# A hybrid encoder layer on one core: modulation matmuls with their operands exchanged, and the stores of summed MLP weight quarters moved from ScalarE's queue to GpSimd's

## The chip, the core and the metric

The kernel is one program on one core of a Trainium2 chip. The time is the device time of one execution in microseconds: 2640.66 us, the median of three runs (2637.92 to 2642.81). A core has five engines that run side by side and meet at semaphores: TensorE (PE; its weight loads are listed as PEld), VectorE (DVE), ScalarE (ACT), GpSimd (POOL) and SyncE (SP), which here only issues DMAs. Each engine takes its instructions strictly in the order in which they stand. DMAs are issued by SP, ACT and POOL.

## The reference

One encoder layer over a prompt of 2048 positions and a sample of 512, width 1024, all in float32:

```
mod = silu(c) @ w_ada + b_ada            # 6 x 1024 values for each of the two requests
shift1, scale1, gate1, shift2, scale2, gate2 = split(mod, 6)
z   = (rmsnorm(x) * (1 + scale1) + shift1) @ w_in
y_f = per-head maps of Re(FFT2(z[:, :512])) + b          # Fourier heads
y_s = GLU(GELU(S5 scan, both ways, of z[:, 512:]))       # state-space heads
x   = x + gate1 * (concat(rmsnorm(y_f), rmsnorm(y_s)) @ w_out)
h   = rmsnorm(x) * (1 + scale2) + shift2
y   = rmsnorm(x + gate2 * (square(relu(h @ w_mlp_in + b)) @ w_mlp_out + b))
```

Two parts matter here. `mod` is a product of a 1024 x 6144 matrix with only two vectors, one per request. The MLP's two products, 1024 x 4096 and 4096 x 1024, are the bulk of the work.

## The kernel before

Most products keep float32 accuracy by splitting both operands into a high and a low part in float32r and adding three products (`mm3`, lines 230 to 232). The modulation, the scan and its outputs use plain float32 matmuls, which the chip runs as two instructions each: the profile shows two records for one matmul in the code.

The stages in order of time, as the profile shows them: the first 2048 columns of the modulation and the parameters of the scan, the input projection and its Fourier folds (to about 340 us); the scan (`Ssm`) with the Fourier transform and its output projection beside it (to about 660 us); the gated unit, the rest of the output projection and the residual (`mix_out`, to about 1010 us); the MLP.

*Modulation slots.* The last 4096 columns of the modulation are 32 blocks j = 16 to 47 of 128 columns. The loop over groups of the scan calls `slot` between its steps; a slot does one block (`ada_slot`, `ada`) and then a unit of the Fourier work. Weights `wa` are loaded two blocks ahead. In `ada`, a block is 8 matmuls (line 688), each with a 128 x 128 block of `w_ada` as the loaded operand and the 128 x 2 tile `cs` of silu(c) as the moved one, summed in a 128 x 2 PSUM tile `pa`; VectorE adds the bias into `mod[:, j]` (line 689). The first 16 blocks are done at the start by `ada1`, with the operands the other way round: `cs` is loaded (two columns), 512 columns of weights are moved (line 706), the 2 x 512 result is copied out by ScalarE into `ar` (line 708) and turned by four small transposes `pat` (line 711).

*Sums of weight quarters.* The MLP uses a scheme of seven products with seven half-size weight matrices for eight. Four of its factors are sums of quarters of a weight matrix, the same in every run but made by the kernel. `precombine` makes one sixteenth of a matrix: SP loads four tiles of 128 x 512 (`in_w`, line 1259), GpSimd makes four sums in place (line 1264), and each sum is stored to `wS` in HBM (line 1265), the store issued by ScalarE. 20 of the 32 calls stand in `mix_out`, with one buffer for each of the four tiles (`q`), and 12 in the first 60 steps of the MLP, in a scratch three calls deep (`big`). The MLP's weight loads `wr` (line 1398) come from the inputs or from `wS`, are cast by ScalarE to high parts `wh` (line 1408), and VectorE makes the low parts `wl` (line 1410).

GpSimd also raises row sums to the power -1/2 for each norm (line 751) and squares the MLP's hidden values (line 1435).

The order in which instructions stand on each engine is set by a scheduler which simulates the program as it is recorded. It works with costs of its own, and its order stands from then on.

Of the kernel before, what the change touches and what calls it, by code (L numbers as in the profile page):

```python
# [9 lines left out]
F32 = mybir.dt.float32  # L10
F32R = mybir.dt.float32r
# [6 lines left out]
LP, LS = 2048, 512  # L18
# [215 lines left out]
def ssm_pre(net, P, pm, side, A, sI, sT, job):  # L234


    nc, tc = net.nc, net.tc
    s4 = [128, NQ, 16, 8]
    flat = lambda t: t.rearrange("p h t -> p (h t)")
    with tc.tile_pool(name="pre1", bufs=1, side=side) as tm, tc.tile_pool(name="pre2", bufs=1, side=side) as tp:  # L240
        T = lambda n, sh=s4, tag=None, bufs=2: tp.tile(sh, F32, tag=tag or n, name=n, bufs=bufs)
        newTh = lambda: tm.tile([128, 2 * NQ, 16, 8], F32, name="Th", bufs=1)
        Th = newTh()
        shf = tm.tile([128, 15, 128], F32R, name="shf")
        net.gate(shf[:1, 0, 0:1])
        nc.gpsimd.dma_start(shf, A["shm"])

        ccs = [{k: T("CC%d%s" % (i, k), [128, NQ, 2, 16], bufs=1) for k in "ri"} for i in range(CB)]
        for cc in ccs:
            for k in "ri":  # L250
                nc.gpsimd.memset(cc[k], 0.0)
        for q in range(32 // NQ):
            gs = slice(q * NQ, q * NQ + NQ)
            if q % 2 == 0:

                Mh = [[tm.tile([128, 2 * NQ, 16], F32R, name="Mh%d%d" % (d, i), bufs=1) for i in range(2)] for d in range(2)]
            ms = slice(q % 2 * NQ, q % 2 * NQ + NQ)
            cc = ccs[q % CB]
            for k, c in (("r", P["Cr"]), ("i", P["nCi"])):
                for d in range(2):  # L260
                    nc.scalar.copy(cc[k][64 * d:64 * d + 64, :, d], c[64 * d:64 * d + 64, gs])
            I = {k: T("I" + k) for k in "ri"}
            pw = {k: bc(P["PWi"][k][:, gs].unsqueeze(2), s4) for k in "ri"}
            bb = {k: bc(P["Bb"][k][:, gs].unsqueeze(3), s4) for k in "ri"}
            for e, k, x, y, op in ((nc.gpsimd, "r", "r", "i", ALU.subtract), (nc.vector, "i", "i", "r", ALU.add)):
                t = T("cb" + k, bufs=1)
                e.tensor_tensor(I[k], bb["r"], pw[x], op=ALU.mult)
                e.tensor_tensor(t, bb["i"], pw[y], op=ALU.mult)
                e.tensor_tensor(I[k], I[k], t, op=op)
            for c, k in enumerate("ri"):  # L270
                It = T("It", [128, NQ, 128])
                ps = net.ps([128, 4, 128], "pst")
                for j in range(4):
                    nc.tensor.transpose(ps[:, j], flat(I[k][:, j]), net.ident)
                nc.scalar.copy(It, ps)
                nc.scalar.dma_start(sI[q, :, c], It)
            ps = net.ps([128, NQ, 2, 16], "psm")
            for j in range(NQ):
                for k in "ri":
                    nc.tensor.matmul(ps[:, j].rearrange("p d h -> p (d h)"), flat(I[k][:, j]), cc[k][:, j].rearrange("p d h -> p (d h)"), start=k == "r", stop=k == "i")  # L280
            M = T("M", [128, 2, NQ, 16])
            Dm = T("Dm", [128, NQ, 16])
            nc.sync.dma_start(Dm, A["s_d"][gs].partition_broadcast(128))
            nc.vector.tensor_tensor(Dm, Dm, bc(P["msk"].unsqueeze(1), [128, NQ, 16]), op=ALU.mult)
            nc.vector.tensor_tensor(M[:, 0], ps[:, :, 0], Dm, op=ALU.add)
            nc.scalar.copy(M[:, 1], ps[:, :, 1])
            for d in range(2):
                split(nc, Mh[d][0][:, ms], Mh[d][1][:, ms], M[:, d])
            job(q)
            for _ in range(2):  # L290
                net.ada_slot()
            if q % 2 == 0:
                continue
            if q > 1:
                Th = newTh()
            for t0 in (0, 4):
                ps = net.ps([128, 4, 2 * NQ, 16], "psT")
                for tau in range(t0, t0 + 4):
                    for d, o in ((0, 14), (1, 7)):
                        for i in range(2):  # L300
                            nc.tensor.matmul(ps[:, tau - t0], shf[:, o - tau], Mh[d][i], start=d + i == 0, stop=d + i == 2)
                nc.scalar.copy(Th[:, :, :, t0:t0 + 4], ps.rearrange("p t g h -> p g h t"))
            for i in range(2):
                nc.scalar.dma_start(sT[q - 1 + i], Th[:, i * NQ:i * NQ + NQ].rearrange("p g h t -> p g (h t)"))


def ssm_out(net, P, tp, q, sO):
# [253 lines left out]
class Net:  # L561
# [3 lines left out]
    def run(self):  # L565
        tc, nc, A = self.tc, self.nc, self.A
        with ExitStack() as es:
# [23 lines left out]
            spps, spp = pool("spp", "right")  # L591
            fes, fe = pool("fe", "right")
            self.Ze = [fe.tile([96, n], F32R, name="Ze%d" % n) for n in (352, 256)]
            self.aj, self.wa = 16, {}
            self.pcs = [(w, c) for w in range(2) for c in range(16)]
            P = self.mix_in(spp)
            sas, sa = pool("ssa", "right")
# [6 lines left out]
            for q in range(nb + 2):  # L604
                if q < nb:
                    bl.append(S.lead(q))
                    self.slot(gen)
                if 1 <= q <= nb:
                    S.step2(bl[q - 1])
                if q >= 2:  # L610
                    self.slot(gen)
                    S.step3(bl[q - 2])
                    self.slot(gen)
                if q < nb:
                    S.step1(bl[q])
                    self.slot(gen)
            self.pull(gen, 1000)
            self.banks(7)
            sps.close()
# [61 lines left out]

    def ada(self, j):
        nc = self.nc
        v3 = lambda n: self.v[n].unsqueeze(2).broadcast_to([128, 8, 2])
        ps = self.ps([128, 2], "pa")
        w = self.wa.pop(j)
        for k in range(8):
            nc.tensor.matmul(ps, w[:, k], self.cs[:, k], start=k == 0, stop=k == 7)  # L688
        nc.vector.tensor_scalar(self.mod[:, j], ps, self.v["b_ada"][:, j:j + 1], None, op0=ALU.add)
        if j == 39:  # L690
            nc.vector.scalar_tensor_tensor(self.gs2, self.mod[:, 32:40], 1.0, v3("g_mlp_norm"), op0=ALU.add, op1=ALU.mult)
        if j == 47:
            nc.vector.tensor_scalar(self.ng2, self.mod[:, 40:48], -1.0, None, op0=ALU.mult)
            nc.vector.tensor_tensor(self.gb2, self.mod[:, 40:48], v3("b_mlp_out"), op=ALU.mult)
# [277 lines left out]
    def fourier(self):  # L972
# [3 lines left out]
        tc, nc, A = self.tc, self.nc, self.A  # L976
        v = nc.vector
        with ExitStack() as es:
            P = lambda n: es.enter_context(tc.tile_pool(name=n, bufs=1))
            tt = P("ft")  # L980
# [3 lines left out]
            CW3 = tp.tile([96, 512], F32R, name="cw3")  # L984
            Z = [t0.tile([128, 4, 352], F32R, name="Z%d" % x) for x in range(2)]
            part = lambda n: tt.tile([128, 516], F32, tag="zin", name="zin", bufs=2)[:, :n]
            zz = t0.tile([128, 94], F32, name="zz")
            v.memset(zz, 0.0)
            for z in Z:
                nc.scalar.copy(z[:, :, 258:352], bc(zz.unsqueeze(1), [128, 4, 94]))  # L990
            lines = [self.fourier_line(tt, tp, CW, CW3, L, ts, Z if L == LP else [t0.tile([128, 1, 352], F32R, name="Zs%d" % x) for x in range(2)], part, zz) for L, ts in self.SEQ]
            def maps():
                wf = tp.tile([128, 4, 128], F32, tag="yF", name="wfo", bufs=YF)
                nc.sync.dma_start(wf, A["w_f"])
# [18 lines left out]
                    else:  # L1013
                        lines.remove(g)

    def fourier_line(self, tt, tp, CW, CW3, L, ts, Z, part, zz):
        nc, A = self.nc, self.A
        v = nc.vector
        q, nt, o = L // 4, len(ts), 128 * 4 * ts[0]
        tag = "p" if L == LP else "s"  # L1020
        T = lambda n, sh, bufs=1, pool=tp: pool.tile(sh, F32R, tag=tag + n, name=n, bufs=bufs)
        if L != LP:
            for z in Z:
                nc.scalar.copy(z[:, 0, 258:352], zz)
        for par in range(2):
# [222 lines left out]
    def precombine(self, pt, bufs=2):  # L1248

        nc = self.nc  # L1250
        if not self.pcs:
            return
        w, c = self.pcs.pop(0)
        A = self.A["w%d" % (w + 1)]
        cc, hf = c // 2, slice(512 * (c % 2), 512 * (c % 2) + 512)
        T = (lambda n, i: pt.tile([128, 512], F32, tag=n, name=n, bufs=bufs)) if not callable(pt) else pt
        a11, a12, a21, a22 = (T(n, i) for i, n in enumerate(("q0", "q1", "q2", "q3")))
        for j, t in enumerate((a11, a12, a21, a22)):
            nc.sync.dma_start(t, A[j, cc, :, hf])
        e = nc.gpsimd  # L1260
        S = self.wS[w]
        for j, o, x, y, op in ((0, a22, a21, a22, ALU.add), (2, a21, a11, a21, ALU.subtract),
                               (1, a11, a22, a11, ALU.subtract), (3, a12, a12, a11, ALU.subtract)):
            e.tensor_tensor(o, x, y, op=op)  # L1264
            nc.scalar.dma_start(S[j, cc, :, hf], o)

    def mlp(self):
        tc, nc, A = self.tc, self.nc, self.A
# [285 lines left out]
```

## Time and profile before

| | |
|---|---|
| median of three runs | 2640.66 us (2637.92 to 2642.81) |
| the profiled execution | 2639.52 us, its span 2637.8 us |
| TensorE busy | 2521.1 us, 96% of the span |
| VectorE, ScalarE busy | 1723.8 us (65%), 1292.3 us (49%) |
| GpSimd busy | 491.3 us (19%) |

Busy time is a share of the span and says nothing of the speed of the work: TensorE's clock has two levels, 1.2 and 2.4 GHz, and the profile gives the granted clock of a stretch as a share of the upper one, so 0.50 is the lower level. An engine's idle time counts only if what it waits for lies on the path to the end. A name like `L688` is line 688 of the kernel; `out<-in` are the tiles it writes and reads; `x16` is the number of records.

### The profile page before, as it was taken

Reading aid. Unit: us, or ns where it says so; the run is one execution under the profiler, and the core shown is the slowest. Engines: PE = TensorE matmul, PEld = TensorE weight load, DVE = VectorE, ACT = ScalarE, POOL = GpSimd, SP = SyncE. Lnnn points to the kernel's source line nnn. Section 1 sums busy time; section 2 is a strip of 40 time slices with the busy share of each in tenths; the row PEclk is TensorE's granted clock in tenths of the full one; section 3 lists DMA queues with packets and bytes.
Section 4 is the critical chain, followed back from the end, with each engine's and each line's share of the span. In section 5 each row is a group of like instructions: output and inputs, shape, how many; then the busy total and the mean of one; then the engine's idle time right before and its main releaser. Section 6 shows DMA issues by size and latency. Waiting matters only on the chain.

```text
span 2637.8 us, 35325 instructions
## 1 busy us (share of the span) xinstructions
PE 2521.1 (96%) x12643; PEld 2280.8 (86%) x12643; DVE 1723.8 (65%) x2839; ACT 1292.3 (49%) x2267; POOL 491.3 (19%) x406
## 2 busy tenths in 40 slices
PE   6789899999989999899999999999999999999997
PEld 2678778778767878799999999999999999999997
DVE  7888778776539767868677877563446442634454
ACT  2643356564524435636544557265445572654443
POOL 4410010000445440951300003013000020130000
PEclk8889978979899999999999999999999999999998
DMA  8644476455678976887666767676667666766664
GB/s 296 204 149 114 138 244 219 166 177 172 210 273 266 310 265 235 291 289 262 235 218 233 270 245 248 234 279 228 228 225 277 243 246 228 274 232 223 224 224 164
DMA packets 274432, 610.53 MB, mean 231 GB/s; under 512 B 66000, under 2 KB 110096, under 8 KB 272464
## 3 DMA queue, kind: packets, MB, share of 16 engines
q1 hardware_dynamic: 233808, 532.35, 59.3%
q10 hardware_dynamic: 34096, 61.32, 6.2%
q0 software_dynamic: 6352, 14.60, 1.7%
q8 instruction: 100, 1.64, 0.2%
q14 instruction: 76, 0.62, 0.1%
HBM read 452.32 MB, written 155.85 MB: 231 GB/s over the span
## 4 chain that ended last, share of the span: by engine, by line
PE 69%; DVE 12%; DMA 9%; ACT 4%; issue 3%; POOL 3%; SPq 0%; ACTq 0%; DVEq 0%; POOLq 0%
PE acc L232 9%; PE acc L231 9%; PE acc L230 9%; PE pf L231 9%; PE pf L230 9%; PE pf L232 9%; PE pa L688 2%; PE psY L383 2%; POOL q L1264 2%; DMA xq<-in_xq 2%; DMA q<-in_w 1%; PE psV L351 1%; DMA wS<-q 1%; PE pof L230 1%; PE pof L231 1%
## 5 line engine op out<-in xcount | busy, mean ns | idle before, releaser
L1408 ACT CAST wh<-wr 128x512 fp32r<-128x512 f32 x672 | 413.7, 620 | 684.9 <-PE acc L231 347.1
L230 PE MATMUL pf<-th,wh 128*128 128x426 f32 (+1 forms) x1344 | 480.6, 358 | 5.0 <-ACT wh L1408 3.9
L232 PE MATMUL pf<-th,wl 128*128 128x426 f32 (+1 forms) x1344 | 476.5, 357 | 8.0 <-DVE wl L1410 8.0
L231 PE MATMUL pf<-th,wh 128*128 128x426 f32 (+1 forms) x1344 | 480.3, 357 | 1.4 <-DVE th L1358 1.4
L231 PE MATMUL acc<-th,wh 128*128 128x426 f32 (+1 forms) x1344 | 478.4, 357 | 0.4 <-DVE th L1358 0.3
L230 PE MATMUL acc<-th,wh 128*128 128x426 f32 (+1 forms) x1344 | 474.5, 357 | 0.0
L232 PE MATMUL acc<-th,wl 128*128 128x426 f32 (+1 forms) x1344 | 466.9, 357 | 2.1 <-DVE wl L1410 2.0
L1428 DVE TENSOR_TENSOR big<-big,pf 128x426 f32<-128x426 f32 (+1 forms) x320 | 184.4, 594 | 179.5 <-PE pf L232 152.9
L1410 DVE TENSOR_TENSOR wl<-wr,wh 128x512 fp32r<-128x512 f32 x288 | 227.2, 800 | 88.4 <-ACT wh L1408 88.0
L1358 DVE TENSOR_TENSOR th<-big,th 128x1704 fp32r<-128x1704 f32 (+1 forms) x82 | 158.7, 1935 | 185.4 <-ACT th L1357 185.2
L232 PEld LDWEIGHTS pf<-th,wl 128*128 128x128 f32 x1344 | 253.0, 188 | 19.2 <-DVE wl L1410 10.5
L230 PEld LDWEIGHTS pf<-th,wh 128*128 128x128 f32 x1344 | 253.0, 188 | 16.0 <-ACT wh L1408 5.3
L232 PEld LDWEIGHTS acc<-th,wl 128*128 128x128 f32 x1344 | 253.1, 189 | 11.2 <-DVE wl L1410 2.8
L231 PEld LDWEIGHTS pf<-th,wh 128*128 128x128 f32 x1344 | 253.6, 189 | 10.1 <-DVE th L1358 1.6
L231 PEld LDWEIGHTS acc<-th,wh 128*128 128x128 f32 x1344 | 252.5, 188 | 9.5 <-DVE th L1358 1.1
L230 PEld LDWEIGHTS acc<-th,wh 128*128 128x128 f32 x1344 | 252.9, 188 | 9.0
L751 POOL TENSOR_TENSOR r<-r,mh 128x4 f32<-128x4 f32 (+3 forms) x32 | 35.5, 1113 | 1140.7 <-DVE r L750 1140.7
L1435 POOL TENSOR_TENSOR big<-big 128x426 f32<-128x426 f32 (+1 forms) x128 | 149.0, 1168 | 466.8 <-ACT big L1434 464.9
L1264 POOL TENSOR_TENSOR q<-q,q 128x512 f32<-128x512 f32 x80 | 140.7, 1758 | 76.3 <-DMA q<-in_w 55.2
L1357 ACT CAST th<-big 128x1704 fp32r<-128x1704 f32 (+1 forms) x82 | 132.5, 1616 | 0.7 <-PE acc L232 0.7
L1358 DVE TENSOR_TENSOR th<-x,th 128x1704 fp32r<-128x1704 f32 (+1 forms) x23 | 46.0, 2001 | 66.3 <-ACT th L1357 66.2
L1434 ACT ACTIVATE big<-big 128x426 f32<-128x426 f32 (+1 forms) x128 | 70.9, 560 | 34.1 <-DVE big L1428 30.5
(444 smaller groups left out, 4445.3 us busy)
## 6 DMA issues: line engine op xcount, KB each, us to landing
wr<-wS SPq DMA_DIRECT2D x192, 512.0 KB, 4.5
wl<-wL SPq DMA_DIRECT2D x192, 512.0 KB, 3.5
wr<-in_w SPq DMA_DIRECT2D x144, 512.0 KB, 4.4
wL<-wl SPq DMA_DIRECT2D x112, 512.0 KB, 2.9
wa<-in_w_ada SPq DMA_DIRECT2D x48, 512.0 KB, 4.5
q<-in_w SPq DMA_DIRECT2D x80, 256.0 KB, 4.2
wS<-q ACTq DMA_DIRECT2D x80, 256.0 KB, 3.8
big<-x1D SPq DMA_DIRECT2D x8, 1704.0 KB, 7.3
```

The lines of the kernel that those rows point to most:

```text
L230: nc.tensor.matmul(out, l[0], r[0], start=start, stop=False)
L231: nc.tensor.matmul(out, l[0], r[1], start=False, stop=False)
L232: nc.tensor.matmul(out, l[1], r[0], start=False, stop=stop)
L383: nc.tensor.matmul(py, m, x[:, j], start=i == 0, stop=i == 2)
L1264: e.tensor_tensor(o, x, y, op=op)
L1357: nc.scalar.copy(th[0], src)
L1358: return th, v.tensor_tensor(th[1], src, th[0].bitcast(F32), op=ALU.subtract)
L1408: nc.scalar.copy(hi, r)
L1410: v.tensor_tensor(lo, r, hi.bitcast(F32), op=ALU.subtract)
L1428: v.tensor_tensor(f[q], f[q], ps, op=op)
L1434: nc.scalar.activation(f[q], f[q], AF.Relu)
L1435: nc.gpsimd.tensor_tensor(f[q], f[q], f[q], op=ALU.mult)
```

## The change

Three edits. In a modulation slot, `cs` is now the loaded operand and the weights are moved, 128 columns a matmul; the 2 x 128 result is copied out by ScalarE into a tile `ar`, and turned by one transpose in the next slot (`ada_turn`), after that slot's eight matmuls; VectorE's add follows there. The last block of the scan's stage is turned by a call behind the loop. The four stores of each `precombine` are issued by the engine that makes the sums, GpSimd. The small tile of zeros that pads the Fourier stage's operands is no longer kept: it is made where it is used, in a buffer that loads of the stage share, which gives the room that `ar` takes.

```
     def ada(self, j):
         nc = self.nc
-        v3 = lambda n: self.v[n].unsqueeze(2).broadcast_to([128, 8, 2])
-        ps = self.ps([128, 2], "pa")
+        ps = self.ps([2, 128], "pa")
         w = self.wa.pop(j)
         for k in range(8):
-            nc.tensor.matmul(ps, w[:, k], self.cs[:, k], start=k == 0, stop=k == 7)
+            nc.tensor.matmul(ps, self.cs[:, k], w[:, k], start=k == 0, stop=k == 7)
+        self.ada_turn()
+        r = self.adp.tile([2, 128], F32, name="ar")
+        nc.scalar.copy(r, ps)
+        self.turn = (j, r)
+
+    def ada_turn(self):
+
+        nc = self.nc
+        if not self.turn:
+            return
+        (j, r), self.turn = self.turn, None
+        v3 = lambda n: self.v[n].unsqueeze(2).broadcast_to([128, 8, 2])
+        ps = self.ps([128, 2], "pat")
+        nc.tensor.transpose(ps, r, self.ident[:2, :2])
         nc.vector.tensor_scalar(self.mod[:, j], ps, self.v["b_ada"][:, j:j + 1], None, op0=ALU.add)
...
             e.tensor_tensor(o, x, y, op=op)
-            nc.scalar.dma_start(S[j, cc, :, hf], o)
+            e.dma_start(S[j, cc, :, hf], o)
...
-            zz = t0.tile([128, 94], F32, name="zz")
-            v.memset(zz, 0.0)
+            def zeros():
+                zz = part(94)
+                v.memset(zz, 0.0)
+                return zz
+            zz = zeros()
```

The order on TensorE early in the scan's stage, before the change; `px` are Fourier products, `psV` and `psY` the scan's, and a row `x11` of `pa` is 11 of a slot's matmuls:

```order
L1055 MATMUL px<-edge,Ze_108 128x128
L688 MATMUL pa<-cs,wa 128x2 x11
L230 MATMUL px<-tab_3341,Zs_3216 128x2
L231 MATMUL px<-tab_3342,Zs_3216 128x2
L232 MATMUL px<-tab_3341,Zs_3217 128x2
L1055 MATMUL px<-edge,Ze_108 128x2
```

And the same place after it:

```order
L1074 MATMUL px<-edge,Ze_108 128x128
L689 MATMUL pa<-wa,cs 2x128 x2
L703 MATMUL pat<-ident,ar 128x2
L689 MATMUL pa<-wa,cs 2x128 x8
L230 MATMUL px<-tab_3343,Zs_3216 128x2
L231 MATMUL px<-tab_3344,Zs_3216 128x2
L232 MATMUL px<-tab_3343,Zs_3217 128x2
L1074 MATMUL px<-edge,Ze_108 128x2
L703 MATMUL pat<-ident,ar 128x2
```

The rest of one slot and a whole one still stand side by side; each is now followed by a transpose of the slot before, and that transpose reads what ScalarE has copied in between.

The order on ScalarE in the first steps of the MLP, before; `wh` are casts of weights, `big` with `pf` reads a product out of PSUM, and each `wS` is a store that waits for GpSimd's sum:

```order
L1440 ACTIVATE big_9176<-pf,vec 128x428
L1265 DMA wS_78<-big_9177 128x512 x2
L1408 CAST wh<-wr 128x512
L1440 ACTIVATE big_9175<-pf,vec 128x428
L1440 ACTIVATE big_9176<-pf,vec 128x428
L1434 ACTIVATE big_9174<-big_9174 128x428
L1265 DMA wS_78<-big_9177 128x512
L1408 CAST wh<-wr 128x512
```

In the changed kernel no store of sums stands on ScalarE; the casts and the reads follow each other alone. The order on GpSimd in `mix_out` in the changed kernel, where one call with its four sums `q` and a power `r` of a norm are shown:

```order
L766 TENSOR_TENSOR r<-r,mh 128x4
L1283 TENSOR_TENSOR q_8181<-q_8180,q_8181 128x512
L1284 DMA wS_77<-q_8181 128x512
L1283 TENSOR_TENSOR q_8180<-q_8178,q_8180 128x512
L1284 DMA wS_77<-q_8180 128x512
L1283 TENSOR_TENSOR q_8178<-q_8181,q_8178 128x512
L1284 DMA wS_77<-q_8178 128x512
L1283 TENSOR_TENSOR q_8179<-q_8179,q_8178 128x512
L1284 DMA wS_77<-q_8179 128x512
L766 TENSOR_TENSOR r<-r,mh 128x4
```

Before the change the same place holds the four sums in a row between the powers; now each sum is followed by its store, which waits for that sum to be written.

## Rows read from the trace of the kernel before

**Rows 1.** The page's busy times: us, share of the span, instructions.

```profile
PE 2521.1 (96%) x12643; PEld 2280.8 (86%) x12643; DVE 1723.8 (65%) x2839; ACT 1292.3 (49%) x2267; POOL 491.3 (19%) x406
```

**Rows 2.** Windows by stage: busy us by engine, granted clock, DMA share, GB/s.

```profile
core 0: us, PE busy (x) PEld busy (x) DVE busy (x) ACT busy (x) POOL busy (x), PEclk, DMA share, GB/s
340.00:660.00 320.00, 313.55 (x1538) 255.26 (x1537) 254.00 (x685) 182.53 (x442) 10.66 (x16) 0.85 0.59 196
660.00:1010.00 350.00, 329.33 (x1437) 266.92 (x1436) 232.46 (x305) 147.24 (x228) 153.17 (x90) 0.95 0.79 263
1010.00:1200.00 190.00, 176.80 (x897) 166.13 (x897) 137.17 (x167) 95.44 (x165) 102.05 (x66) 0.99 0.81 279
```

**Rows 3.** Timeline of TensorE, two slot runs: start, length, line, tiles, records.

```profile
407.27 2.79 PE L688 MATMUL pa<-cs,wa 128*128 128x2 f32 x24
...
613.05 1.84 PE L688 MATMUL pa<-cs,wa 128*128 128x2 f32 x16
```

**Rows 4.** Windows of 2 us around those runs.

```profile
408.00:410.00 2.00, 2.00 (x20) 2.00 (x19) 2.00 (x6) 0.00 (x0) 0.28 (x1) 1.00 1.06 357
412.00:414.00 2.00, 2.00 (x6) 1.31 (x5) 2.00 (x6) 1.99 (x11) 0.00 (x0) 0.50 1.14 398
613.00:615.00 2.00, 2.00 (x18) 1.96 (x18) 1.93 (x5) 0.59 (x1) 0.00 (x0) 1.00 0.15 57
```

**Rows 5.** Windows of 20 us around two idle gaps of TensorE.

```profile
336.00:356.00 20.00, 17.39 (x53) 12.75 (x54) 12.14 (x34) 15.26 (x53) 4.19 (x8) 0.57 1.10 350
546.00:566.00 20.00, 17.95 (x63) 13.88 (x64) 13.67 (x37) 9.15 (x27) 0.00 (x0) 0.66 0.37 120
```

**Rows 6.** The first modulation blocks: one run in the timeline, two windows.

```profile
16.62 7.03 PE L706 MATMUL pa<-wa,cs 128*2 128x512 f32 x16
...
28.00:30.00 2.00, 2.00 (x3) 0.26 (x2) 1.51 (x11) 1.15 (x2) 0.00 (x0) 0.50 1.02 340
32.00:34.00 2.00, 2.00 (x6) 0.33 (x4) 2.00 (x9) 0.63 (x2) 0.00 (x0) 1.00 1.03 397
```

**Rows 7.** The maps' products between slot pieces: timeline, window.

```profile
391.60 1.14 PE L1000 MATMUL pc<-wfo,zin 128*128 128x128 f32 x8
...
390.00:392.00 2.00, 2.00 (x20) 2.00 (x19) 2.00 (x8) 0.79 (x3) 0.00 (x0) 1.00 0.81 279
```

**Rows 8.** The first blocks' transposes (timeline) and copies (line, ns min/median/max).

```profile
16.31 0.38 PE L711 MATMUL pat<-ident,ar 2*128 2x2 f32 x4 [0.76 <-ACT ar L708]
...
L708 ACT COPY ar<-pa x4: 557/572/574, 15.6 to 50.3; 2x512 f32<-2x512 f32 x4
```

**Rows 9.** GpSimd: one DMA issue (timeline); windows of the sums, then of squares.

```profile
48.42 0.54 POOL L246 DMA_DIRECT2D shf<-in_shm  x1
...
660.00:1010.00 350.00, 140.66 (x80) 0.95 0.79 263
1056.00:1176.00 120.00, 79.23 (x48) 0.99 0.86 301
...
1056.00:1176.00 120.00, 21.58 (x16) 0.99 0.86 301
```

**Rows 10.** Waits: waiter, releaser: us in total, times, longest (660-1200; 1010-1200; 660-1010).

```profile
ACT wh L1408 <- POOL big L1264: 21.3, 9, 4.6
ACT wh L1408 <- DMA wS<-big: 19.6, 4, 7.1
...
PE pf L232 <- DVE wl L1410: 6.8, 6, 1.8
...
PE pgate L230 <- ACT of L1143: 6.4, 1, 6.4
...
SPq L1259 <- DMA wS<-q: 58.3, 37, 5.5
```

**Rows 11.** DMA issues: queue, count, KB each, median us to landing.

```profile
wS<-q ACTq DMA_DIRECT2D x80, 256.0 KB, 3.8
...
edge<-in_f_edge POOLq DMA_DIRECT2D x1, 192.0 KB, 8.8
```

More of the change, by code (lines that the diff above doesn't have):

```diff
@@ L304, in ssm_pre @@
                 nc.scalar.dma_start(sT[q - 1 + i], Th[:, i * NQ:i * NQ + NQ].rearrange("p g h t -> p g (h t)"))
+        net.ada_turn()
 def ssm_out(net, P, tp, q, sO):
@@ L593, in run @@
             self.Ze = [fe.tile([96, n], F32R, name="Ze%d" % n) for n in (352, 256)]
-            self.aj, self.wa = 16, {}
+            self.aj, self.wa, self.turn = 16, {}, None
             self.pcs = [(w, c) for w in range(2) for c in range(16)]
@@ L683, in ada @@
         nc = self.nc
[L684 to L685 removed]
+        ps = self.ps([2, 128], "pa")
         w = self.wa.pop(j)
         for k in range(8):
[L688 removed]
+            nc.tensor.matmul(ps, self.cs[:, k], w[:, k], start=k == 0, stop=k == 7)
+        self.ada_turn()
+        r = self.adp.tile([2, 128], F32, name="ar")
[9 more added lines that the diff above has]
+        nc.tensor.transpose(ps, r, self.ident[:2, :2])
         nc.vector.tensor_scalar(self.mod[:, j], ps, self.v["b_ada"][:, j:j + 1], None, op0=ALU.add)
@@ L986, in fourier @@
             part = lambda n: tt.tile([128, 516], F32, tag="zin", name="zin", bufs=2)[:, :n]
-            zz = t0.tile([128, 94], F32, name="zz")
-            v.memset(zz, 0.0)
+            def zeros():
[3 more added lines that the diff above has]
+            zz = zeros()
             for z in Z:
                 nc.scalar.copy(z[:, :, 258:352], bc(zz.unsqueeze(1), [128, 4, 94]))
-            lines = [self.fourier_line(tt, tp, CW, CW3, L, ts, Z if L == LP else [t0.tile([128, 1, 352], F32R, name="Zs%d" % x) for x in range(2)], part, zz) for L, ts in self.SEQ]
+            lines = [self.fourier_line(tt, tp, CW, CW3, L, ts, Z if L == LP else [t0.tile([128, 1, 352], F32R, name="Zs%d" % x) for x in range(2)], part, zeros) for L, ts in self.SEQ]
             def maps():
@@ L1014, in fourier, with fourier_line @@
                         lines.remove(g)
-    def fourier_line(self, tt, tp, CW, CW3, L, ts, Z, part, zz):
+    def fourier_line(self, tt, tp, CW, CW3, L, ts, Z, part, zeros):
         nc, A = self.nc, self.A
@@ L1022, in fourier_line @@
         if L != LP:
+            zz = zeros()
             for z in Z:
```

## The prediction

> **What bounds the kernel now.** I read the page's busy times first, then the windows by stage, then the waits of the stages that the change touches. TensorE is the bound nearly throughout: 2521.1 of 2637.8 us [rows 1]. The windows say how it is bound [rows 2]. In 340 to 660 us, where all 32 modulation slots stand, TensorE is busy 313.55 of 320 us, but its granted clock averages 0.85, so a share of that busy time is work at the lower level, 1.2 GHz. VectorE is second there, 254.00 us. In 660 to 1010 and 1010 to 1200, where GpSimd sums the MLP quarters, TensorE stands idle 20.7 and 13.2 us at clocks of 0.95 and 0.99. What a slot and a store cost is therefore read from these stages alone; after 1200 us nothing is edited.
>
> The reader should see one thing in the small windows. From 407.27 to about 410.1 us TensorE runs 24 records of slot matmuls without a gap [rows 3], the window is full (2.00 of 2.00), the clock is 1.00 in it, and 0.50 in 412 to 414, again with no idle time [rows 4]. So the clock fell although TensorE never stood still, directly behind slot work. One slot alone between full-width matmuls, 16 records in 1.84 us at 613.05, leaves the clock at 1.00 [rows 3, 4].
>
> **The slots.** A slot is 8 matmuls, 16 records, that load a 128x128 block of weights and move two columns. Turned, it loads two columns and moves 128. The shortfall of clock in the stage is 320 x (1 - 0.85) = 48 us of full-speed time. Not all of it is the slots': two low stretches begin at an idle gap of TensorE, and their rows give 20 x 0.43 + 20 x 0.34 = 8.6 + 6.8 = 15 us [rows 5]. What is left, 33 us, I put down to slot runs, as at 412 us; this is an attribution from that pattern and not from a row for each stretch. Does the turned form keep the clock? The first modulation blocks already have that form (two columns loaded, 512 moved): at 28 to 30 us they run at 0.50, and at 32 to 34 us, TensorE doing little but them, at 1.00 [rows 6]. So two loaded columns do not keep the clock down. For a length of 128 the row is the maps' matmuls (128 loaded, 128 moved), eight of them at 391.60 between slot pieces, and the window of 390 to 392 stays at 1.00 [rows 7].
>
> The page "TensorE: Matmul & The Clock Gate" of the Trainium skill (Part 1: The HAM clock gate) says that the gate follows how busy the engine has lately been and that idle stretches throttle it. By that rule alone a slot without gaps would cost no clock, and turning it would return none; the trace disagrees, with 0.50 behind a full window [rows 4]. That outcome is rival one below; by the rule the sum would be its 2643.5 us.
>
> Of the 33 us I take two thirds, 22. The limit is VectorE: with 33 us gone TensorE needs 313.6 - 33 = 281 us, and VectorE's 254 us would be 90% of it, up from 79% of 320, so some of the gain turns into waits for VectorE's sweeps. The ends are 0 (VectorE takes it all, or the clock does not come back) and 48 (the idle gaps' part goes too).
>
> What the slots cost at full speed hardly moves. Now 16 records take 1.84 us, 0.115 us each with the tail of the last [rows 3]. The 512-column form takes 7.03 us for 16, 0.44 each [rows 6]; a quarter of the columns gives 0.11 us, an estimate from that row. The upper end is the maps' form, eight in 1.14 us [rows 7], 0.14 each or 2.28 us a slot, +0.44. So 32 slots change by +1 us (-5 to +14). Added are 32 transposes: four took 0.38 us [rows 8], under 0.1 each: +3 us (+2 to +5). Added are also 32 copies of a 2x128 tile on ScalarE; the 2x512 one took 0.57 us [rows 8], so below 18 us in all on an engine that is busy 182.53 of 320 us [rows 2]: hidden by its own idle time. A new wait comes with them, TensorE's transpose for that copy. The transpose stands behind the next slot's eight matmuls, 1.7 us later, which covers 0.57 us; what queues behind it on TensorE is the sweeps' matmuls. ScalarE is in order and may come late: +2 us (0 to +15). The second PSUM tile per slot shares four banks; its cost is in that range. The moved zero tile is one more memset on VectorE: nothing, hidden under matmuls, +-1 if not.
>
> Slots: -22 + 1 + 3 + 2 = -16 us.
>
> **The stores.** 128 issues leave ScalarE's queue. What they did there is to hold ScalarE until GpSimd's sum was ready or an earlier store had landed: in 660 to 1200 its weight casts alone waited 21.3 us for GpSimd and 19.6 us for stores [rows 10]. Behind those casts VectorE and then TensorE wait: 6.8 us in 1010 to 1200 for the low parts; and in 660 to 1010 TensorE waited 6.4 us at once for ScalarE's output copy [rows 10]. I take 6 of the 6.8 and 4 of the 6.4, and keep 0 and all 13.2 as the ends. Late next there is VectorE's subtraction itself.
>
> What they do on GpSimd: one issue by GpSimd took 0.54 us [rows 9]. 48 of them in 1056 to 1176 us add 26 us to 79.23 + 21.58 = 101 us of sums and squares in 120 us: 127 us, more than there is. Queued behind the issues are the next sums, then SyncE's loads into the same scratch, then the weight loads behind those on SyncE. Overrun 7 us; scratch three quarters deep hides half: +3 (0 to +7). In 660 to 1010 the 80 issues add 43 us to 140.66 us of 350 [rows 9]: room, but the reciprocal roots of the row norms stand between them, and each can come up to a store later.
>
> Then the landing. A 256 KB store from ScalarE's queue lands in 3.8 us; from GpSimd's queue the trace has loads only, 192 KB in 8.8 us, at a busy time [rows 11]. So a store lands -1 to +5 us later; the end below nothing is there because a store no longer stands in ScalarE's queue behind other work. SyncE waited 58.3 us, 37 times, for these stores before it could reload a tile [rows 10], with loads and stores of other tiles queued behind. 37 x (-1 to +5) is -37 to +185 us of SyncE's wait; a ninth of the present wait reaches TensorE (6.4 of 58.3, the output copy whose store was queued there). That gives -4 to +20; I take +5, nearer to the queue's better case since DMA is less full here than at 340 us.
>
> Stores: -6 - 4 + 3 + 5 = -2 us (-17 to +27).
>
> The page "SBUF — State Buffer" of the Trainium skill (SBUF: two separate sides) warns that VectorE in its two-port modes keeps GpSimd from writing its descriptors, so that a DMA from that queue starts late. No row here shows such a delay. By that rule the landing would tend to the late end, +20 instead of +5; that is rival two's direction.
>
> **Sum.** -16 - 2 = -18 us. The profiled execution took 2639.52 us (span 2637.8 and 1.7 around it), 1.1 us under the median of three runs, 2640.66. 2639.5 - 18 = 2621.5; I say 2621. The work between 340 and 1200 us also stands in another order, since the scheduler was fed other costs; I give that +-6 us and no sign.
>
> **Rivals.** One: the clock does not pay. Either the turned slots do not hold it, or VectorE, full in the windows at 408 and at 412 us [rows 4], takes the place of TensorE. For it: 2.00 of 2.00 us busy there. Against it: the first blocks and the maps [rows 6, 7], and that VectorE has a fifth of the stage free [rows 2]. Time: the new costs stay and the gain goes, 2639.5 + 6 - 2 = 2643.5, between 2634 and 2650.
>
> Two, slower: the stores bind on GpSimd. Place: the sums' loop, load, sum, store, reload, with SyncE's queue behind it. Price: +20 from landings of 8.8 us and +7 from the overrun, less 4 us saved in 660 to 1010, +23; the 6 us in 1010 to 1200 are not saved, because the weights come late. For it: GpSimd has no room in 1056 to 1176 [rows 9], and the only landing of that size from its queue [rows 11]. Against it: that landing was a load at a busy time. It decides where the price passes the slots' 16 us: 16 + 4 - 7 = 13 us of landings, at 37 / 9 = 4 us for each microsecond of delay about 3 us, so from a landing of 7 us on. With all of the slots' gain it ends at 2639.5 - 16 + 23 = 2646.5, with half of their 22 us at 2657.5.
>
> Three: more than I take. The full 33 us and stores at -13, the price of landings and overrun at 0: 2639.5 - 33 + 6 - 13 = 2599.5.
>
> **How the numbers follow.** The forecast has 0.55, with 2607 to 2634 as its own range. Rival one has 0.18, rival two 0.17, rival three 0.10. A measurement here tells 0.2%, 5.3 us, from no change. Faster than 2635.4: all of 0.55 and 0.10, a quarter of rival one, 0.05, and a little of two, 0.02: 0.72. Within 0.2%: half of rival one, 0.09, and 0.03 of two: 0.12. Slower: 0.16. The range of 8 in 10 leaves out the lower half of rival three and the upper half of two: 2598 to 2648.
>
> **What would show it.** Clock: the granted clock of the slots' stage should rise from 0.85 to above 0.93, with no window at 0.50 behind a slot run, and the stage should be about 15 us shorter; a clock near 1 with TensorE waiting for VectorE is rival one's second half. Slots: 0.11 us from start to start, and waits for the copy of 2 us or less in sum. Stores: no wait of a cast for GpSimd or a store; issues near 0.54 us; landings under 6 us. The forecast is wrong if the clock in that stage stays under 0.9, or if the two stages after it are longer by more than 5 us together.

## The result and the profile after

The changed kernel takes 2665.23 us (median of four runs, 2659.81 to 2671.9), the kernel before 2640.99: a ratio of 1.0094, 95% interval 1.0076 to 1.0111, so 0.9% slower. That lies outside the range given, 2598 to 2648, and on the other side of no change. The profiled execution took 2667.35 us.

The page's busy times, then the windows by stage (columns as in [rows 2]):

```profile
PE 2515.3 (94%) x12675; PEld 2246.4 (84%) x12675; DVE 1775.6 (67%) x2840; ACT 1300.1 (49%) x2299; POOL 535.4 (20%) x534
```

```profile
340.00:660.00 320.00, 302.95 (x1610) 220.62 (x1607) 250.87 (x677) 187.22 (x465) 12.36 (x15) 0.98 0.60 193
660.00:1010.00 350.00, 311.72 (x1345) 249.63 (x1345) 246.55 (x294) 136.85 (x208) 177.32 (x167) 0.94 0.76 251
1010.00:1200.00 190.00, 166.62 (x809) 155.00 (x808) 155.67 (x153) 92.17 (x159) 113.78 (x112) 0.93 0.74 254
```

Against [rows 1, 2]: in the slots' stage the clock rose from 0.85 to 0.98, and TensorE now idles 17 us there instead of 6.5. In the two stages of the sums TensorE does less in the same stretch (329.33 to 311.72, 176.80 to 166.62 us), and VectorE is busy longer with fewer instructions (137.17 us for 167, now 155.67 for 153). Where the loss falls shows in the start times of a few products (us; the kernel with the slots alone is the first experiment below):

| start of | before | slots alone | both |
|---|---|---|---|
| scan, last output product | 650.9 | 655.7 | 652.9 |
| gated unit, first product | 758.5 | 745.6 | 741.4 |
| output projection, last product | 1013.0 | 1010.2 | 1023.9 |
| MLP, first product | 1014.4 | 1012.1 | 1033.3 |
| MLP, second layer, first product | 1298.0 | 1295.4 | 1322.6 |

TensorE comes to the gated unit 17 us early, 13 of them with the slots alone, and has lost 42 us against that when the second layer starts.

The slots' own rows, all of the changed kernel: two slots in the timeline, the windows of 2 us behind them, then another pair and what follows it, the copies, and TensorE's idle time before transposes (us, times):

```profile
427.09 1.91 PE L689 MATMUL pa<-wa,cs 128*2 128x128 f32 x16
429.47 1.91 PE L689 MATMUL pa<-wa,cs 128*2 128x128 f32 x16 [0.31 <-DVE mod L704]
```

```profile
431.00:433.00 2.00, 1.50 (x9) 1.04 (x7) 1.15 (x5) 1.89 (x7) 0.00 (x0) 1.00 0.57 203
433.00:435.00 2.00, 2.00 (x10) 1.41 (x8) 1.97 (x6) 0.40 (x2) 0.00 (x0) 1.00 0.78 271
```

```profile
547.65 1.91 PE L689 MATMUL pa<-wa,cs 128*2 128x128 f32 x16
551.38 0.22 PE L703 MATMUL pat<-ident,ar 2*128 2x2 f32 x1 [1.82 <-ACT ar L692]
```

```profile
554.00:556.00 2.00, 2.00 (x5) 1.20 (x5) 1.93 (x6) 0.25 (x1) 0.00 (x0) 0.50 0.32 91
```

```profile
L692 ACT COPY ar<-pa x32: 237/254/256, 342.0 to 655.4; 2x128 f32<-2x128 f32 x32
...
  ACT ar L692: 2.6, 2
```

A slot takes 1.91 us where it took 1.84 [rows 3], the clock stays at 1.00 behind the 32 records from 427.09 on, and the new wait costs 2.6 us. These costs came out within their ranges. The clock does not hold everywhere: the pair that ends at 549.56 is followed by the wait for the copy, 1.82 us of idle TensorE, and by 0.50 in 554 to 556.

GpSimd's stores, from the DMA issues (columns as in [rows 11]), and VectorE's subtraction for the weights' low parts in 1010 to 1210 us (count, busy us, mean ns, idle before) in the changed kernel:

```profile
wS<-q POOLq DMA_DIRECT2D x80, 256.0 KB, 4.0
...
wS<-big POOLq DMA_DIRECT2D x48, 256.0 KB, 3.9
```

```profile
L1429 DVE TENSOR_TENSOR wl<-wr,wh 128x512 fp32r<-128x512 f32 x68 | 94.8, 1402 | 14.2 <-ACT wh L1427 14.1
```

The stores land in 4.0 us, as from ScalarE (3.8, [rows 11]). The subtraction takes 1402 ns; with the slots turned and the stores on ScalarE it takes 942:

```profile
L1429 DVE TENSOR_TENSOR wl<-wr,wh 128x512 fp32r<-128x512 f32 x75 | 70.1, 942 | 25.3 <-ACT wh L1427 25.0
```

### The profile page after: what moved, and what is told of

Read it like the earlier page. It is cut to its first block, busy times and chain, and to the rows that moved or that the text cites. A ratio compares the mean times of both kernels' runs of the same rounds, so it can differ in the third digit from the quotient of the medians.

```text
span 2665.5 us, 35392 instructions
## 1 busy us (share of the span) xinstructions
PE 2515.3 (94%) x12675; PEld 2246.4 (84%) x12675; DVE 1775.6 (67%) x2840; ACT 1300.1 (49%) x2299; POOL 535.4 (20%) x534
## 4 chain that ended last, share of the span: by engine, by line
PE 54%; DVE 10%; DMA 5%; issue 2%; POOL 1%; ACT 1%; SPq 0%; DVEq 0%; ACTq 0%; POOLq 0%
PE acc L232 9%; PE acc L231 9%; PE acc L230 9%; PE pf L232 9%; PE pf L231 9%; PE pf L230 9%; DVE wl L1429 2%; DMA q<-in_w 2%; DMA wS<-q 1%; POOL q L1283 1%; DMA xo<-in_xT 1%; DVE big L1447 1%; DVE x L1495 1%; DVE xo L1240 1%; DVE mg L227 1%
## 5 line engine op out<-in xcount | busy, mean ns | idle before, releaser
L1429 DVE TENSOR_TENSOR wl<-wr,wh 128x512 fp32r<-128x512 f32 x288 | 254.2, 893 | 78.5 <-ACT wh L1427 78.0
L1283 POOL TENSOR_TENSOR q<-q,q 128x512 f32<-128x512 f32 x80 | 122.8, 1535 | 117.8 <-DMA q<-in_w 96.9
```

Of the source, the lines that this page charges most:

```text
L1429: v.tensor_tensor(lo, r, hi.bitcast(F32), op=ALU.subtract)
```

## The experiments

Ratios are to the kernel before in the same session, with 95% intervals. "Slots" is the changed kernel with the stores left on ScalarE.

### One edit at a time

`e1_slots`:

```
-            e.dma_start(S[j, cc, :, hf], o)
+            nc.scalar.dma_start(S[j, cc, :, hf], o)
```

> The slots turned, the zero tile moved, the stores of the sums left on ScalarE. In the changed kernel the output projection's last Fourier product started 11 us earlier than before and the MLP 23 us later, so the loss lies in the stages where the sums are stored. Theory A (the stores on GpSimd cost, the slots gain): 2617 to 2630 us, the granted clock of the slots' stage near 0.98, and the MLP's first products 10 us or more earlier than before. Theory B (the slots' gain is given back later by the new order of the work, and the stores cost nothing): 2655 us or more.

Measured: 2634.5 us, 0.9982 (0.9966 to 0.9998). `callable(pt)`, in edits below, is true in the MLP's steps and false in the output projection's stage. `e2_stores` is the kernel before with the stores on GpSimd alone.

> The slots as before, only the stores of the sums moved to GpSimd. Theory A: 2670 to 2690 us, with VectorE's subtraction for the low parts (0.97 us a record on average before in 660 to 1210 us) at 1.3 us or more. Theory B: 2636 to 2646 us, and that subtraction under 1.05 us.

Measured: 2658.5 us, 1.0066 (1.0044 to 1.0087). `e3_mixout`:

```
-            e.dma_start(S[j, cc, :, hf], o)
+            (nc.scalar if callable(pt) else e).dma_start(S[j, cc, :, hf], o)
```

> The changed kernel with the 48 stores of the MLP's first steps back on ScalarE; the 80 in the output projection's stage stay on GpSimd. Theory A, cost in proportion to where VectorE's instructions grew (20 us in the output projection's stage, 31 us in the MLP's): about 2640 to 2650 us. If the whole cost comes from the late start of the MLP, that is from the 80 stores: 2655 to 2668. Theory B: no change, 2660 to 2668.

Measured: 2665.0 us, 1.0089 (1.0059 to 1.0119). `e4_sync` has `nc.sync` there.

> The changed kernel with all 128 stores issued by SyncE, so that GpSimd makes the sums alone, as before the change. Theory A (what costs is GpSimd issuing the stores, through VectorE): VectorE's subtraction is back under 1.05 us, and the time lies between 2617 and 2645, the upper part if SyncE's loads wait behind stores that wait for sums. Theory C (what costs is that ScalarE no longer paces the sums, so that they run at once and hit VectorE harder, whoever issues): VectorE's subtraction stays at 1.3 us or more, and the time above 2650.

Measured: 2635.7 us, 0.9981 (0.9969 to 0.9993). So the stores on GpSimd are what costs: 0.7% alone, 1.1% on top of the slots; theory B falls, and C with it, since SyncE's stores cost nothing. Theory A's sizes were missed: the slots gain 0.2% instead of reaching 2617 to 2630 us, the MLP starts 2 us earlier and not 10, and `e2_stores` stays under 2670 us. With 20 calls the 80 stores of the output projection's stage bear the price. Whether the 48 of the MLP bear none was tried directly with `h2_mlp_stores`, which swaps the two engines of `e3_mixout`:

> The slots turned; only the 48 stores in the MLP's first steps on GpSimd, the 80 of the output projection's stage on ScalarE. From the stretch between the first products of the MLP's two layers (283.3 us with the stores on ScalarE, 289.3 with them on GpSimd): 6 us more than with all on ScalarE, 2637 to 2646 us, with VectorE's subtraction for the low parts at 1.3 us on average in the first 200 us of the MLP. If these stores cost nothing: 2630 to 2637.

Measured: 2638.5 us, 0.9975 (0.9960 to 0.9990). The microseconds lie at the edge of both ranges; the ratio, taken in its own session, is as good as with none there. Yet VectorE's subtraction is at 1233 ns in it: longer instructions of VectorE by themselves are not a price.

```profile
L1429 DVE TENSOR_TENSOR wl<-wr,wh 128x512 fp32r<-128x512 f32 x76 | 93.5, 1233 | 16.8 <-ACT wh L1427 16.7
```

### Is it the loop of load, sum, store, reload?

Two buffers for each tile, with the stores on ScalarE (`f1_slots_two`), on GpSimd (`f2_after_two`), and in the kernel before (`f4_before_two`):

```
-                            self.precombine(tp, 1)
+                            self.precombine(tp, 2)
```

> The slots turned, the stores on ScalarE (2634.5 us so far), and two buffers instead of one for each of the four tiles of the sums in the output projection's stage. Theory L (the loop of load, sum, store and reload paces that stage, so part of the slots' gain was given back there, and the stores on GpSimd cost because they make the loop longer): the stage no longer waits for the loop, and the time is 2618 to 2628 us. Theory P (what costs is the port that GpSimd and VectorE share, and the loop paces nothing): 2630 to 2640 us.

> The changed kernel, stores on GpSimd (2665 us so far), with the same two buffers. Theory L: the stores cost little once a reload needn't wait for them, 2620 to 2642 us. Theory P: VectorE is held up as before, 2655 us or more.

> The kernel before with two buffers for the sums' tiles, as a control for the slots' gain without the loop. Theory L: since TensorE reached that stage 13 to 20 us later here than with turned slots, the loop held it less; 2632 to 2641 us, and the kernel with turned slots and two buffers is faster than this one by 12 to 20 us. Theory P: within 6 us of the kernel before, and the difference between the two stays at the 7 us seen so far.

Measured: 2658.9 us, 1.0056 (1.0036 to 1.0076); 2657.3 us, 1.0055 (1.0036 to 1.0075); 2644.6 us, 1.0001 (0.9985 to 1.0017). Theory L's figures fail, and for the first run theory P's too: with two buffers and turned slots the last sum comes 40 us earlier, and the stage gets longer all the same. The scheduler orders everything anew when a buffer is added, so these runs change more than the loop; why the first of them lost 20 us wasn't settled. Between the first two the stores on GpSimd cost nothing, though VectorE is busy 459 instead of 426 us from the gated unit to the second layer.

Loads of the sums' tiles taken off SyncE's queue, for the output projection's stage, with the stores on ScalarE (`g3_slots_gload`) and on GpSimd (`g4_after_gload`):

```
-            nc.sync.dma_start(t, A[j, cc, :, hf])
+            (nc.sync if callable(pt) else nc.gpsimd).dma_start(t, A[j, cc, :, hf])
```

> The slots turned, the stores on ScalarE, the 80 loads of the sums' tiles in the output projection's stage issued by GpSimd instead of SyncE. Theory S: SyncE's queue no longer stands still for stores, 2615 to 2632 us. Theory P: GpSimd writes descriptors for loads instead, and VectorE is held up as with its stores: 2645 us or more.

> The changed kernel with these loads on GpSimd too, so that load, sum and store all stand in GpSimd's queue. Theory S: faster than the changed kernel by 15 us or more, 2620 to 2650 us, and the first load of the row norms for the MLP (1018.5 us after, 990.6 with the stores on ScalarE) is issued before 1000 us. Theory P: GpSimd writes twice as many descriptors in that stage, 2665 to 2700 us.

Measured: 2643.5 us, 1.0014 (0.9996 to 1.0032), and 2705.4 us, 1.0239 (1.0219 to 1.0258). The first lies between the ranges. Theory S is not borne out: a SyncE queue without these loads gains nothing, though GpSimd has 80 issues more here; and `e4_sync`, with 128 more issues on SyncE, loses nothing. The second is useful for another reason. Its last sum starts at 1060.7 us, and the MLP starts at 1083.5, 59 us behind the output projection's last product (1024.6).

### GpSimd's time, or its stores?

`f3_fill` gives GpSimd about the time of an issue without a store, 0.74 us a sum. A store takes 0.56 us and, before it, 0.30 us of waiting for its sum:

```
-            e.tensor_tensor(o, x, y, op=op)
+            s = e.tensor_tensor(o, x, y, op=op)
             nc.scalar.dma_start(S[j, cc, :, hf], o)
+            if not callable(pt):
+                with self.tc.issue_after(s.ins):
+                    e.memset(pt.tile([128, 768], F32, tag="fill", name="fill", bufs=1), 0.0)
```

> The slots turned, the stores on ScalarE, and after each of the 80 sums of the output projection's stage a fill of an unused 128x768 tile by GpSimd, about 0.6 us, which takes GpSimd's time as a store's issue does, reads nothing and writes no descriptor. Theory L (GpSimd's time between the sums lengthens the loop): 2655 to 2670 us, and VectorE's instructions no longer than with the stores on ScalarE alone. Theory P (the descriptors take the port): 2632 to 2642 us.

Measured: 2646.5 us, 1.0019 (1.0006 to 1.0032): 0.4% over the slots alone, about 10 us, between the two theories. GpSimd's time alone, at this length, is a third of the price. `h3_mlp_fill` does the same beside the MLP's 48 sums, in a free part of their scratch:

> The slots turned, all stores on ScalarE, and beside each of the 48 sums in the MLP's first steps a fill of an unused 128x704 tile by GpSimd, about 0.6 us. If GpSimd's time is what costs there, about the same 6 us as its stores, 2637 to 2646 us; if it is the hold on VectorE, which a fill that reads nothing doesn't give, 2630 to 2637 us and VectorE's subtraction as with the stores on ScalarE alone.

Measured: 2636.6 us, 0.9977 (0.9962 to 0.9992): nothing, as the stores there. `h4_after_late` writes the four stores behind the four sums:

```
             e.tensor_tensor(o, x, y, op=op)
-            e.dma_start(S[j, cc, :, hf], o)
+        for j, o in ((0, a22), (2, a21), (1, a11), (3, a12)):
+            e.dma_start(S[j, cc, :, hf], o)
```

> The changed kernel with the four stores of a call written behind its four sums, so that most of them are issued one sum later and none waits 0.3 us for the sum before it: about 80 x 0.3 = 24 us less of GpSimd's time in the loop. If GpSimd's time sets the loop (of 69 us added by the stores, 34 showed in its length), the last sum comes about 12 us earlier, near 1001 us, the MLP starts within 20 us of it, and the time is 2650 to 2660 us. If the hold on VectorE is what costs, it stays at 2660 to 2670.

Measured: 2665.4 us, 1.0070 (1.0048 to 1.0092). Not told from the changed kernel. The loop did not get shorter (last sum at 1016.2 us), so the run doesn't test what it was made for.

### The split between the stages

`g1_slots_14` (stores on ScalarE), `g2_after_14` (on GpSimd), `h1_before_14` (slots as before): `PCG = 20`, the number of calls in the output projection's stage, becomes 14. `i1_slots_17`, `i2_after_17`: 17.

> The slots turned, the stores on ScalarE, with 14 of the 32 calls that make sums in the output projection's stage instead of 20, the other 18 in the MLP's first steps. Two buffers in place of one made this kernel slower (2659), so the loop by its reload alone is not what paces the stage. Theory S (SyncE's in-order queue: loads of the sums' tiles wait there for stores to land, and the stage's own loads stand behind them): fewer calls, less of that, 2615 to 2632 us. Theory O (chance of the order that the scheduler gives): no forecast, 2625 to 2660.

> The changed kernel, stores on GpSimd, with 14 calls in the output projection's stage. Theory S: the loop now ends well ahead of the stage's last block, and the price of the stores on GpSimd falls from 30 us to under 15 against the same kernel with the stores on ScalarE. Theory P (the port shared by VectorE and GpSimd): the price goes with the number of stores, 20 us or more. Theory O: the difference may have either sign.

> The kernel before with 14 calls of sums in the output projection's stage instead of 20 (with turned slots: 2645.6 us, its last output product at 1000.1 us). If the loop of sums is what takes back the slots' gain, then with a loop that ends early the gain is whole: this kernel ends 12 to 18 us later than that one, 2656 to 2664 us, its last output product at 1010 us or later. If the gain is lost elsewhere: 6 to 9 us later, 2650 to 2655.

> The slots turned, the stores on ScalarE, 17 calls of sums in the output projection's stage and 15 in the MLP's first steps: the control for the next run. Between 20 calls (2634.5 us) and 14 (2645.6): 2634 to 2644 us.

> The changed kernel with 17 calls. The last sum of the output projection's stage comes near 965 us, far enough ahead of the MLP, and the MLP's 60 stores lie between 48, which cost nothing, and 72, which cost 14 us in its first steps. Theory G (the sums take longer, and that costs only where their end is waited for): 8 to 16 us over the kernel with 17 calls and the stores on ScalarE, less than with 14 calls (22) or 20 (31). Theory P (each store holds VectorE): 22 to 31 us over it, as with 14 and 20.

Measured: 2645.6 us, 1.0019 (1.0009 to 1.0029); 2667.4 us, 1.0099 (1.0082 to 1.0117); 2654.4 us, 1.0036 (1.0021 to 1.0051); 2639.4 us, 0.9990 (0.9976 to 1.0003); 2670.4 us, 1.0105 (1.0084 to 1.0125). The price of the stores is 0.8% with 14 calls and 1.15% with 17, as theory P has it: it does not go away where the MLP no longer starts behind the last sum (1018.0 against 974.1 us with 17), so theory G falls as the only cause. It moves, though: with 17 calls, and 60 stores in the MLP, most of it lies in the MLP's first layer. That the MLP's stores are free holds for the 48. The slots' gain is 0.2% with 14 calls as with 20, so the loop isn't what eats it either.

In the last pair the waits show where the time goes. TensorE's waits for VectorE (waiter, releaser: us, times, longest) in 735 to 1340 us, with the stores on ScalarE and then on GpSimd:

```profile
PE pf L232 <- DVE wl L1429: 5.4, 6, 1.7
PE pn L752 <- DVE ss L1249: 5.1, 3, 3.1
PE pn L752 <- DVE ss L1174: 2.6, 1, 2.6
```

```profile
PE pf L232 <- DVE wl L1429: 16.8, 6, 5.3
PE pn L752 <- DVE ss L1249: 14.6, 3, 6.9
PE pn L752 <- DVE ss L1174: 4.7, 2, 4.3
```

## Why the prediction was wrong

**What the 30 us are.** From the gated unit's first product to the second layer's first, slots alone, then the changed kernel, then the fill, one window each:

```profile
746.00:1295.00 549.00, 518.26 (x2462) 457.09 (x2461) 415.65 (x546) 257.04 (x422) 241.08 (x169) 0.98 0.82 273
```

```profile
741.00:1323.00 582.00, 528.00 (x2466) 465.59 (x2467) 460.06 (x547) 259.47 (x424) 297.81 (x285) 0.95 0.77 259
```

```profile
743.00:1302.00 559.00, 525.79 (x2464) 463.35 (x2465) 421.58 (x546) 258.36 (x422) 290.59 (x235) 0.96 0.80 269
```

The same work takes 33 us longer: 23 us more of idle TensorE (30.7 to 54.0) and 10 us more of busy time at a lower clock (0.98 to 0.95). By the start times of products, in us:

| | gated unit's first to output projection's last | on to the MLP's first | on to the second layer's first |
|---|---|---|---|
| slots alone | 264.6 | 1.9 | 283.3 |
| fill | 280.7 | 0.2 | 278.4 |
| 80 stores on GpSimd (`e3_mixout`) | 277.9 | 12.5 | 282.0 |
| changed kernel | 282.5 | 9.4 | 289.3 |
| 17 calls, stores on ScalarE | 263.1 | 2.6 | 288.0 |
| 17 calls, stores on GpSimd | 272.3 | 1.3 | 306.7 |

In the output projection's stage the fill costs nearly what the stores cost; it does not delay the MLP, and part of its loss comes back there.

VectorE does the same instructions, 546 and 547, in 460 instead of 416 us. That is not the price itself: in `e3_mixout`, as slow as the changed kernel, it is 428 us. What goes with the price is TensorE's waiting for VectorE. In these windows such waits add up to 17.7 us with the slots alone and 14.8 with the fill, but to 32.4 in `e3_mixout` (748 to 1320 us) and 39.5 in the changed kernel. The stores also stretch VectorE's instructions more than a fill does: beside the same 80 sums 428 us against 421.58, and beside the MLP's 48 sums 1233 ns a subtraction (`h2_mlp_stores`) against 1020 (`h3_mlp_fill`) and 942 with neither. The fill holds GpSimd a little less long than a store with its wait does, and how much of the difference comes of that was not measured. The largest waits, slots alone and then changed; the ones for `th` and `of` are for ScalarE:

```profile
PE pn L752 <- DVE ss L1249: 7.4, 2, 5.2
PE pf L232 <- DVE wl L1429: 6.3, 4, 3.0
...
PE pout L231 <- DVE mg L227: 0.9, 1, 0.9
```

```profile
PE pn L752 <- DVE ss L1249: 15.2, 3, 8.1
PE pf L232 <- DVE wl L1429: 11.9, 5, 3.4
PE pf L230 <- ACT th L1376: 9.0, 1, 9.0
PE pout L231 <- DVE mg L227: 4.7, 2, 4.1
...
PE pgate L230 <- ACT of L1162: 0.7, 1, 0.7
```

**How a store holds VectorE.** Timeline of the changed kernel, VectorE and then GpSimd (`pf` of line 1240 is a tile in SBUF):

```profile
995.45 2.27 DVE L1240 SCALAR_TENSOR_TENSOR xo<-pf,mod,xo 128x512 f32<-128x512 f32 x1 [1.31 <-DMA xo<-in_xT]
997.64 4.03 DVE L227 TENSOR_TENSOR mg<-ys,mg 128x512 fp32r<-128x512 f32 x4
1001.60 0.74 DVE L1240 SCALAR_TENSOR_TENSOR xo<-pf,mod,xo 128x512 f32<-128x512 f32 x1
```

```profile
995.31 0.56 POOL L1284 DMA_DIRECT2D wS<-q  x1 [0.30 <-POOL q L1283]
995.88 1.27 POOL L1283 TENSOR_TENSOR q<-q,q 128x512 f32<-128x512 f32 x1
997.45 0.56 POOL L1284 DMA_DIRECT2D wS<-q  x1 [0.30 <-POOL q L1283]
998.03 1.27 POOL L1283 TENSOR_TENSOR q<-q,q 128x512 f32<-128x512 f32 x1
```

The instruction of 995.45 became ready while GpSimd issued a store. It took 2.27 us; the same line at 1001.60, with GpSimd idle, took 0.74. Its end, 997.72, lies 0.57 us behind the end of the sum that began after it, at 995.88. The next one, of 997.64, again begins within an issue. So in this place an instruction of VectorE that came up during an issue let the next sum go first, and TensorE's product with `mg` waited 4.1 us. Sums without stores hold this line too; with the slots alone it took 1.78 us beside four of them:

```profile
980.63 1.78 DVE L1240 SCALAR_TENSOR_TENSOR xo<-pf,mod,xo 128x512 f32<-128x512 f32 x1
```

```profile
977.10 6.46 POOL L1283 TENSOR_TENSOR q<-q,q 128x512 f32<-128x512 f32 x4 [4.60 <-issue]
```

The mean over the stage, slots alone and changed, of this line, of the one that updates `xo` from PSUM and of the one that makes `mg`:

```profile
L1240 DVE SCALAR_TENSOR_TENSOR xo<-pf,mod,xo 128x512 f32<-128x512 f32 x34 | 32.9, 972 | 17.3 <-DMA xo<-in_xT 12.7 <-DMA pf<-pD 4.5
...
L1244 DVE SCALAR_TENSOR_TENSOR xo<-pout,mod,xo 128x512 f32<-128x512 f32 x33 | 24.2, 739 | 3.0 <-PE pout L232 2.5 <-DVE xo L1240 0.5
...
L227 DVE TENSOR_TENSOR mg<-ys,mg 128x512 fp32r<-128x512 f32 x20 | 12.6, 677 | 0.0
```

```profile
L1240 DVE SCALAR_TENSOR_TENSOR xo<-pf,mod,xo 128x512 f32<-128x512 f32 x34 | 33.0, 971 | 15.1 <-DMA xo<-in_xT 7.5 <-DMA pf<-pD 4.1 <-issue 3.5
...
L1244 DVE SCALAR_TENSOR_TENSOR xo<-pout,mod,xo 128x512 f32<-128x512 f32 x34 | 25.1, 741 | 2.6 <-PE pout L232 2.5
...
L227 DVE TENSOR_TENSOR mg<-ys,mg 128x512 fp32r<-128x512 f32 x20 | 19.4, 1010 | 0.0
```

The line that reads PSUM is not held at all (739, 741). Of those with both operands in SBUF `mg` grows (677 to 1010 ns), and line 1240 is as long beside the sums alone (972, 971); another line, 1226, even gets shorter (1104 to 892). So the stores' hold falls on some instructions and passes by others. The page "SBUF — State Buffer" of the Trainium skill (Who interferes with whom) says that an instruction of VectorE with two SBUF inputs contends with a GpSimd instruction that reads SBUF, and that one with a single SBUF input, outside the two-port modes, does not; the trace agrees on these three lines. The same section has it that whoever starts first goes first; there the trace differs by its start times, since the sum of 995.88 went ahead of an instruction that had stood since 995.45.

**The MLP's start.** It is a second way, seen where the last sum is late. The MLP's first row norms are loaded into memory that the sums' tiles free, so their load waits for the last store, and the products follow some 21 us behind the last sum (last start of the sums, first start of the MLP's products). Changed kernel, then with the loads on GpSimd:

```profile
L1283 POOL TENSOR_TENSOR q<-q,q x80: 1268/1301/4005, 689.8 to 1011.9; 128x512 f32<-128x512 f32 x80
...
L230 PE MATMUL pf<-th,wh x1344: 349/357/724, 1033.3 to 2383.1; 128*128 128x426 f32 x128, 128*128 128x428 f32 x64
...
SPq L1338 <- DMA wS<-q: 0.9, 1, 0.9
```

```profile
L1283 POOL TENSOR_TENSOR q<-q,q x80: 1249/1302/3555, 693.1 to 1060.7; 128x512 f32<-128x512 f32 x80
...
L230 PE MATMUL pf<-th,wh x1344: 349/357/695, 1083.5 to 2423.0; 128*128 128x426 f32 x128, 128*128 128x428 f32 x64
```

In `e3_mixout` and `h4_after_late` it is 1016.8 to 1038.4 and 1016.2 to 1038.5. With the slots alone the last sum starts at 981.9 and the MLP follows the output projection at once, at 1012.1. The wait that shows it is TensorE's 9.0 us for `th` above.

**Step by step.** *Bound, and clock behind slots*: right in the main; the stage's clock of 0.98 beats the 0.93 asked for, with a window at 0.50 left behind one pair of slots. *"Of the 33 us I take two thirds"*: the clock came back and its worth did not. The slots' -16 us measured -5. With them alone TensorE is 13 us early at the gated unit and 3 at the output projection's end (10 with 14 calls); from the one to the other it takes 264.6 us instead of 254.5, and 7.5 of the 10 are idle time. The reason given, waits for VectorE's sweeps, is not what the rows show: in 340 to 660 us TensorE waits for VectorE about 2 us in all and for ScalarE 12, so this is not rival one's second half either. *New costs of the slots*: right, but the copy's wait of 2.6 us is over the 2 asked for. *"In 660 to 1010 the 80 issues add 43 us to 140.66 us of 350: room"*: this step failed. It counted GpSimd's room and not who waits beside it. The 80 sums before took 140.66 us [rows 9], 1.76 each, where one alone takes 1.27 to 1.30: that something held them stood in the row, and I read a busy time from it. The stores' term, -2, measured +30 on the turned slots and +17 on the old ones; -5 and +30 make the measured +24. TensorE's waits for VectorE and the MLP's late start, for which the sum had no term, stand in its place. *What the stores held on ScalarE*: the waits went as forecast (the 6.4 us of TensorE for `of` are 0.7 now), and the waits for VectorE, late next, grew by more than that. *The landing*: 4.0 us, at the good end; it cost nothing. *The MLP's 48 stores*, the overrun of 7 us: wrong place; there the 48 stores cost nothing. *Rival two* had the sign, the engine and a time not far off (2657.5 at its upper end), but its price was landings of 8.8 us, which were not there, and its point of decision, 7 us, was never reached. Its loop did get longer, the last sum coming 30 us later than with the slots alone, by GpSimd's issues and not by landings; so its time is near by luck. The page “SBUF — State Buffer” of the Trainium skill, as weighed there, has VectorE delay GpSimd's descriptors. Here GpSimd's stores delayed VectorE.

**What stays open.** How the 30 us divide between the hold and the late start of the MLP: with 17 calls the MLP's start isn't bound and the price is the same, with 20 it is. The hold is seen in single places, not summed into the price, and a fill as long as a store with its wait was not run. Where the slots' gain goes behind the gated unit is not settled, nor why two buffers made the turned kernel slower.

The best version that ran is the changed kernel without its second edit, 2634.5 us (0.9982); with the stores issued by SyncE it is the same (0.9981), and both beat the kernel before by 0.2% and the one after by 1.1%.

## What to carry to other kernels

A DMA moved to GpSimd can be paid by those who wait for VectorE and for GpSimd's last result: before giving GpSimd issues among its own instructions, look at which VectorE instructions with two SBUF operands run beside them, who waits for those, and what starts behind the last of GpSimd's work. Room in an engine's busy time says nothing of what its neighbours lose. A higher clock in one stage need not reach the end (here 13 us at the gated unit, 5 in the time): ask which product's start time it moves at the end of the next stage, not how much busy time it saves.

## What was not expected of the hardware

A VectorE instruction that came up during GpSimd's issue of a store waited for the rest of the issue and the whole next sum (2.27 us against 0.74 with GpSimd idle; beside sums alone 1.78). In the MLP's first steps seven subtractions, each 0.68 us at its shortest, took 17.40 us in a row:

```profile
1066.57 17.40 DVE L1429 TENSOR_TENSOR wl<-wr,wh 128x512 fp32r<-128x512 f32 x7 [1.65 <-ACT wh L1427]
```

A fill by GpSimd of 0.68 us beside the same sums (`h3_mlp_fill`) did nothing of the kind: no subtraction in 1010 to 1210 us took longer than 1.86 us, where the longest in the changed kernel took 5.85. With the stores on GpSimd its own sums run faster: the MLP's take 1.30 us (median), with the slots alone 1.63.
